# Two-block transformer kernel: the second block's residual in pairs of feature tiles, the sum of squares ahead of the next products, and two moved modulation loads

## The chip, the cores and the metric

The kernel runs on one core of one Trainium2 chip. The metric is device time in microseconds (us), the median over runs. The engines are named as in the profile: PE is TensorE (PEld its weight loads), DVE is VectorE, ACT is ScalarE, POOL is GpSimd, SP is SyncE, which here only issues transfers.

## The reference

512 tokens of 1024 features (and 256 context tokens in the first block) pass through two blocks of two layers, all in fp32. The first block has attention, a Fourier mixer and a Hyena mixer, then a squared-ReLU MLP. The second block, cut to what the change touches, is per layer:

```python
mixed = rms_norm_2(mixer(modulate(rms_norm_2(h, g0), shift, scale)), g1)   # mixer ends in a product with w_out
h = h + gate * mixed
f = rms_norm_2(swiglu_ffn(modulate(rms_norm_2(h, g2), shift2, scale2)), g3)
h = h + gate2 * f
```

where rms_norm_2(x, g) = x * rsqrt(mean(x*x) + 1e-6) * g over the 1024 features. So behind each of the four big products of the second block stands the same tail: a mean of squares of the product y, a residual x + y * gain * r with gain = g * gate per feature and r = rsqrt per token, and a second mean of squares, now of the new x, for the norm ahead of the next product. Layer 0's mixer is HGRN2, layer 1's is dilated attention.

## The kernel before, in words

Activations are feature-major: x is [128 partitions, 8 feature tiles, 512 tokens]. An fp32 product is three matmuls on parts of the operands (mm3: hi by hi at L153, hi by lo at L154 or L155, lo by hi). A weight chunk of 128 x 1024 is loaded raw by SP (wchunk, 3 buffers), its hi part is cast by ACT (L118), its lo part is a subtraction (L119) on POOL, or on DVE for some chunks.

`gemm` takes the output feature tiles m = 0..7 as "head" outputs, once for each part of the tokens: 0:256 and 256:512 (HALVES), or 0:512 and 512:768 in the first block where the context follows the tokens (SEGS). In the first part it takes outputs two at a time, with the eight k steps of the two interleaved, so both chunks' lo parts are wanted almost at once; in a later part, where a function `after` is given, one at a time. `after(s, e)` returns the steps that follow a finished part; they are put on a list, `self.chain`, and `self.link(3)` runs three of them behind each output of the next part. So the first step of a part (`first`: a matmul with a matrix of ones that sums the squares over the partitions, L314, then Ln, Exp, Square on ACT, L318 to L322, and two DVE instructions, L323 and L324, which give r) is emitted behind the first output of the next part. `self.bg(n)` runs n background steps behind an output: loads (L418), products (L424) and finishes (transposes at L433) of the modulation vectors; `bg_flush` runs all that are left.

The order that each engine gets is made from this order of emission by a planner with its own model of durations: an instruction that the model holds ready may be placed ahead of one that it holds not ready. On the chip each engine then runs its list in order.

`resid2` makes the tail of the second block: `first`, then for each of the 8 feature tiles one DVE instruction y * gain * r into a scratch tile (L1340), one add to x (L1341; in the last layer POOL adds tiles 0, 3 and 6), and for the next norm an ACT Square (L290, or L286 for the first) and a DVE add into a running sum (L291). `norm2` follows with three empty steps, its own `first` (of x) and 8 modulate steps (L333, L342, L343), which write the next product's operand u. `proj_out` is the mixer's last product (evacuated by an ACT copy, L1358); `ffn2` ends in `ff_wout` in three chunks of k, of which the last (c == 2) has `after`.

In the first block the first `win` gemm carries background loads and products of modulation vectors in a list that `mod_products` spaces by a gap (3 at L945). The attention output product of layer 0 (`project`, w_out, SEGS) has such a list too, one load of 1 MB (tile mp_w) for each quarter; before it, `load_x` issues the reload of x and of the context from L1065 and L1067.

Of the kernel before, what the change touches and what calls it, by code (L numbers as in the profile page):

```python
# [13 lines left out]
AF = mybir.ActivationFunctionType  # L14
ALU = mybir.AluOpType
# [3 lines left out]
P = 128  # L19
D = 1024  # L20
KD = D // P
L = 512
C = 256
# [56 lines left out]
class Kern:  # L80
# [90 lines left out]
    def gemm(self, srcs, nk, rhs, segs, evac, head=2, parts=None, after=None, n=1024, bg=0, lead=2, dep=False):  # L171

        srcs = list(srcs)
        seg = segs if callable(segs) else (lambda m: segs)
        parts = [(x,) for x in parts] if parts else [seg(0)]
        short = self.xring is None and parts[-1][-1][1] - parts[-1][0][0] <= C

        load = lambda m, short=False: self.wchunk(
            srcs[m], n, extra=self.xring is not None and m > 2,
            lo_eng=self.nc.vector if dep or short and m % 3 == 2 else None)
        head = min(head, len(srcs))
        keep = None  # L190
        if self.xring is not None:

            order = sorted(range(head), key=lambda m: (m not in (3, 4, 5), m)) if dep else range(head)
            keep = {m: load(m) for m in order}
        for part in parts if head else ():
            if dep and part is not parts[0]:
                self.link()
            m0 = 0
            while m0 < head:
                g = lead if m0 == 0 and part is parts[0] else 1 if after and part is not parts[0] else 2  # L200
                ms = range(m0, min(m0 + g, head))
                m0 = ms[-1] + 1
                ws = [keep[m] if keep else load(m, short and part is parts[-1]) for m in ms]
                outs = [[self.psa()[:, : e - s] for s, e in part] for _ in ms]
                for k in range(nk):
                    for w, oo in zip(ws, outs):
                        for (s, e), o in zip(part, oo):
                            self.mm3(o, w[:, k * P : (k + 1) * P], rhs(k)[:, s:e], k == 0, k == nk - 1)
                for m, oo in zip(ms, outs):
                    for (s, e), o in zip(part, oo):  # L210
                        evac(m, s, e, o)
                    if (after or part is parts[-1]) and not (dep and len(parts) > 1):
                        self.bg(bg)
                    self.link(3)
            if after:
                self.link()
                for s, e in part:
                    self.chain += after(s, e)
        for m in range(head, len(srcs)):
            if dep:  # L220
                self.link()
            for (s, e), o in zip(seg(m), self.mtile(self.wchunk(srcs[m], n), nk, rhs, seg(m))):
                evac(m, s, e, o)
            self.bg(bg)
# [662 lines left out]
    def block1_layer(self, l):  # L887
        nc, a = self.nc, self.a
        last = l == 1
# [17 lines left out]
        else:  # L907
# [7 lines left out]
            hvp = ues.enter_context(self.pool("hv", "right"))  # L915
# [26 lines left out]
                      lambda m, s, e, ps: evac(lo + m, s, e, ps), bg=3, **kw)  # L942

        if not last:
            fl, self.bgq = self.bgq, self.mod_products(hvp, "w_mod0", self.bmod[0], (self.m1[0], self.mc[0]), range(2, 4), 3,  # L945
                                                    (hvp, "mp_a"))
            for i, step in enumerate(fl):
                self.bgq.insert(3 * i + 3 * (i > 0), step)
            win(0, 8, tok, evac_hyena, parts=SEGS)
            wes.close()  # L950
            mid = lay.enter_context(self.pool("mid"))
# [14 lines left out]
        if last:  # L966
            hvp = ut
# [57 lines left out]
        else:  # L1025
            p, cat = open_cat()
# [42 lines left out]
        if not last:  # L1069
# [9 lines left out]
            for k in range(4):  # L1079
# [3 lines left out]
            p = tmp.enter_context(self.pool("mods", "right"))  # L1083
            self.bgq += self.mod_products(p, "w_mod0", self.bmod[0], (self.m1[0], self.mc[0]), range(4, 5), 3,
                                          (self.stp, "st_r"))

            def after(s, e):
                if s > 0:
# [231 lines left out]

        return self.norm_to(self.stp, ("b2", l, j), s, self.ng[l][:, 2 * j * KD : (2 * j + 1) * KD], self.m2[l], 3 * j, s, e, LAG)

    def resid2(self, l, j, p, y, sty, s, e):

        nc = self.nc
        last = l == 1 and j == 1
        v = {}

        def first():
            o = (3 * j + 2) * KD  # L1330
            v["r"] = self.stat_rstd(self.stp, sty, D)
            v["g"] = self.cached_gain(("res", l, j), self.ng[l][:, (2 * j + 1) * KD : (2 * j + 2) * KD],
                                      self.m2[l][:, o : o + KD])
            if not last:
                self.st[s] = self.stat_new(self.stp, e - s)

        def tile(k):
            t = self.t(p, [P, C], "r2_t", 3 if last else 2)[:, : e - s]
            x = self.xk(k, s, e)
            nc.vector.scalar_tensor_tensor(t, y[:, k, s:e], v["g"][:, k : k + 1], v["r"], op0=ALU.mult, op1=ALU.mult)  # L1340
            (nc.gpsimd if last and k % 3 == 0 else nc.vector).tensor_tensor(x, x, t, op=ALU.add)  # L1341
            if not last:
                self.stat_add(self.stp, self.st[s], x)
            elif k % 2:
                nc.sync.dma_start(self.a["out"][:, k - 1 : k + 1, s:e], self.x[:, k - 1 : k + 1, s:e])

        return [first] + [lambda k=k: tile(k) for k in range(KD)]

    def proj_out(self, l, key, p, cat):

        nc = self.nc
        y = self.t(p, [P, KD, L], "y")
        sty = {}

        def evac(m, s, e, ps):
            if m == 0:
                sty[s] = self.stat_new(self.stp, e - s)
            nc.scalar.copy(y[:, m, s:e], ps)  # L1358
            self.stat_add(self.stp, sty[s], ps)

        def after(s, e):
            return self.resid2(l, 0, p, y, sty[s], s, e) + self.norm2(l, 1, s, e)

        self.gemm([self.a[key][m] for m in range(KD)], KD, lambda k: cat[k], FULL, evac,
                  head=KD, parts=HALVES, after=after)
        self.link(1 + KD)
# [417 lines left out]
    def ffn2(self, l, es_x):  # L1784
        nc, a = self.nc, self.a
        with self.pool("hid") as hp, self.pool("y") as yp:
# [15 lines left out]
            def evac_out(m, s, e, ps):  # L1802
                if c == 0:
                    nc.scalar.copy(y[:, m, s:e], ps)
                else:
                    nc.vector.tensor_tensor(y[:, m, s:e], ps, y[:, m, s:e], op=ALU.add)
                if c == 2:
                    if m == 0:
                        sty[s] = self.stat_new(self.stp, e - s)
                    self.stat_add(self.stp, sty[s], y[:, m, s:e])  # L1810

            def after(s, e):
                self.bg_flush()
                steps = self.resid2(l, 1, hp, y, sty[s], s, e)
                return steps + self.norm2(1, 0, s, e) if l == 0 else steps

            m0 = 0
# [238 lines left out]
```

## Time and profile before

| what | value |
| --- | --- |
| median of 3 runs | 3510.9 us (3509.56 to 3512.11) |
| the profiled execution | 3506.06 us |
| its span | 3504.3 us |
| instructions | 46813 |
| PE busy | 3287.6 us, 94% of the span |
| DVE, ACT, POOL busy | 57%, 37%, 35% |
| HBM traffic | 106 GB/s over the span |

In the rows further down, a timeline row is: start in us, busy us, engine, line, operation, output<-inputs, shape, count of like instructions that it stands for, and in brackets how long the engine was idle before it and what released it. Starts are from the span's start. A row of the waits says engine, line, what it waited for: us in total, times, longest. "PEclk" is the granted clock of TensorE as a share of full speed.

### The profile page before, as it was taken

Reading aid. Unit: us, or ns where it says so; the run is one execution under the profiler, and the core shown is the slowest. Engines: PE = TensorE matmul, PEld = TensorE weight load, DVE = VectorE, ACT = ScalarE, POOL = GpSimd, SP = SyncE. Lnnn points to the kernel's source line nnn. Section 1 sums busy time; section 2 is a strip of 40 time slices with the busy share of each in tenths; the row PEclk is TensorE's granted clock in tenths of the full one; section 3 lists DMA queues with packets and bytes.
Section 4 is the critical chain, followed back from the end, with each engine's and each line's share of the span. In section 5 each row is a group of like instructions: output and inputs, shape, how many; then the busy total and the mean of one; then the engine's idle time right before and its main releaser. Section 6 shows DMA issues by size and latency. Waiting matters only on the chain. (4 is left out here: it accounts for less than half of the span.)

```text
span 3504.3 us, 46813 instructions
## 1 busy us (share of the span) xinstructions
PE 3287.6 (94%) x18400; PEld 2757.6 (79%) x18400; DVE 2013.0 (57%) x3173; ACT 1288.1 (37%) x2260; POOL 1212.6 (35%) x635
## 2 busy tenths in 40 slices
PE   6988888999998989999999898999989999999998
PEld 2766667888887667888888778888888888898887
DVE  5437748574556557757775666476585474461224
ACT  3235634121123346532245555222423323352222
POOL 2424432222224444234432341344313333313443
PEclk9999999999999999999999999999999999999999
DMA  6330034343433310235542123455323223322332
GB/s 201 127 106 20 29 125 138 109 123 119 133 114 111 98 56 25 90 119 182 185 141 94 55 67 112 150 183 183 100 78 102 91 79 97 97 89 86 95 92 72
DMA packets 150912, 374.32 MB, mean 107 GB/s; under 512 B 18939, under 2 KB 40482, under 8 KB 150692
## 3 DMA queue, kind: packets, MB, share of 16 engines
q1 hardware_dynamic: 146468, 367.14, 32.8%
q10 hardware_dynamic: 4224, 4.19, 0.4%
q8 instruction: 145, 2.38, 0.3%
q14 instruction: 75, 0.61, 0.1%
HBM read 364.98 MB, written 6.29 MB: 106 GB/s over the span
## 5 line engine op out<-in xcount | busy, mean ns | idle before, releaser
L119 POOL TENSOR_TENSOR w_l<-wr,w_h 128x1024 fp32r<-128x1024 f32 (+1 forms) x381 | 915.2, 2404 | 1900.7 <-ACT w_h L118 1891.3
L153 PE MATMUL A<-u_h,w_h 128*128 128x512 f32 (+1 forms) x2344 | 873.6, 374 | 14.5 <-ACT u_h L118 5.0
L155 PE MATMUL A<-u_h,w_l 128*128 128x512 f32 (+1 forms) x2344 | 866.1, 370 | 8.0 <-DVE w_l L119 6.6
L154 PE MATMUL A<-u_l,w_h 128*128 128x512 f32 (+1 forms) x2344 | 866.9, 370 | 1.7 <-DVE u_l L119 1.0
L118 ACT CAST w_h<-wr 128x1024 fp32r<-128x1024 f32 (+1 forms) x406 | 420.3, 1037 | 1100.8 <-PE A L154 745.3
L153 PEld LDWEIGHTS A<-u_h,w_h 128*128 128x128 f32 x2344 | 444.5, 190 | 105.1 <-issue 8.0
L155 PEld LDWEIGHTS A<-u_h,w_l 128*128 128x128 f32 x2344 | 445.2, 190 | 90.6 <-DVE w_l L119 7.7
L154 PEld LDWEIGHTS A<-u_l,w_h 128*128 128x128 f32 x2344 | 445.2, 190 | 82.1 <-DVE u_l L119 1.7
L155 PE MATMUL A<-hid_h,w_l 128*128 128x512 f32 (+1 forms) x1072 | 376.1, 351 | 8.6 <-POOL w_l L119 8.6
L154 PE MATMUL A<-hid_l,w_h 128*128 128x512 f32 (+1 forms) x1072 | 377.6, 352 | 3.1 <-DVE hid_l L119 3.1
L153 PE MATMUL A<-hid_h,w_h 128*128 128x512 f32 (+1 forms) x1072 | 378.6, 353 | 1.4 <-ACT hid_h L118 1.4
L387 DVE SCALAR_TENSOR_TENSOR mo_a<-mo_w,mc_c,mo_a 128x512 f32<-128x512 f32 x266 | 278.4, 1047 | 81.0 <-DMA mo_w<-in_ada_dram 53.4
L155 PEld LDWEIGHTS A<-hid_h,w_l 128*128 128x128 f32 x1072 | 202.8, 189 | 38.5 <-POOL w_l L119 10.7
L154 PEld LDWEIGHTS A<-hid_l,w_h 128*128 128x128 f32 x1072 | 203.2, 190 | 30.9 <-DVE hid_l L119 4.4
L153 PEld LDWEIGHTS A<-hid_h,w_h 128*128 128x128 f32 x1072 | 203.1, 189 | 29.5 <-ACT hid_h L118 2.2
L1799 DVE TENSOR_TENSOR sg<-A,sg 128x512 f32<-128x512 f32 (+1 forms) x52 | 31.4, 607 | 242.6 <-PE A L155 210.0
L1182 DVE SCALAR_TENSOR_TENSOR x<-A,m,x 128x512 f32<-128x512 f32 (+1 forms) x96 | 61.9, 658 | 189.3 <-PE A L155 189.3
L1130 DVE TENSOR_TENSOR relu<-relu 128x512 f32<-128x512 f32 (+1 forms) x104 | 81.3, 810 | 83.9 <-ACT relu L1129 83.9
L1631 DVE TENSOR_TENSOR qk<-A,cos 128x512 f32<-128x512 f32 (+1 forms) x56 | 47.1, 841 | 130.5 <-PE A L155 130.3
L153 PE MATMUL A<-w_h,u_h 128*128 128x256 f32 (+1 forms) x408 | 119.7, 293 | 2.1 <-DVE rt L1634 2.1
L154 PE MATMUL A<-w_l,u_h 128*128 128x256 f32 (+1 forms) x408 | 119.8, 294 | 0.0
L155 PE MATMUL A<-w_h,u_l 128*128 128x256 f32 (+1 forms) x408 | 118.8, 291 | 0.0
(559 smaller groups left out, 6066.0 us busy)
## 6 DMA issues: line engine op xcount, KB each, us to landing
wr<-in_w_mlp_dram SPq DMA_DIRECT2D x139, 512.0 KB, 3.9
mo_w<-in_ada_dram SPq DMA_DIRECT2D x192, 256.0 KB, 2.9
wr<-in_ff_win_dram SPq DMA_DIRECT2D x88, 512.0 KB, 3.7
mo_w<-in_w_mod_dram SPq DMA_DIRECT2D x112, 256.0 KB, 2.8
wr<-in_at_wqk_dram SPq DMA_DIRECT2D x48, 512.0 KB, 3.5
wr<-in_ff_wout_dram SPq DMA_DIRECT2D x32, 512.0 KB, 3.5
wr<-in_w_in_dram SPq DMA_DIRECT2D x30, 512.0 KB, 3.5
mp_w<-in_w_mod_dram SPq DMA_DIRECT2D x12, 1024.0 KB, 5.6
```

The lines of the kernel that those rows point to most:

```text
L118: nc.scalar.copy(dst.hi, src)
L119: (lo_eng or nc.vector).tensor_tensor(dst.lo, src, dst.hi.bitcast(F32), op=ALU.subtract)
L153: ins = mm(out, lhs.hi, rhs.hi, start=first, stop=False)
L154: mm(out, lhs.hi, rhs.lo, start=False, stop=False)
L155: mm(out, lhs.lo, rhs.hi, start=False, stop=last)
L387: nc.vector.scalar_tensor_tensor(state[i], raw, cc[:, k : k + 1], state[i], op0=ALU.mult, op1=ALU.add)
L1130: nc.vector.tensor_tensor(r, r, r, op=ALU.mult)
L1182: nc.vector.scalar_tensor_tensor(x, ps, mod[:, o : o + 1], x, op0=ALU.mult, op1=ALU.add)
L1631: nc.vector.tensor_tensor(d, vw(ps), vw(c), op=ALU.mult)
L1799: nc.vector.tensor_tensor(sgs[s], ps, sgs[s], op=ALU.mult)
```

## The change

The second block's residual takes two feature tiles an instruction and works in y's own place: y *= r (r broadcast over the two tiles), x += y, Square of x into y, and the sum of squares over the pairs, with one 256-wide add at the end; the scratch tile is gone, and the last layer's adds are all on DVE. The gain is applied earlier, when y is evacuated: as the scale of the ACT copy in `proj_out`, and as one more ACT instruction in place in `ffn2`'s last chunk; the table that Ln and Exp use is asked for at the first evacuation. In `gemm`, outputs with `after` are taken one at a time in the first part too (the first group is still `lead`, two), and one chain step is run right behind `after`. In the first `win` the gap of `mod_products` is 2, and in layer 0's `project` the first background step, a load of mp_w, is run ahead of the gemm.

```diff
--- before.py
+++ after.py
@@ -197,7 +197,7 @@
                 self.link()
             m0 = 0
             while m0 < head:
-                g = lead if m0 == 0 and part is parts[0] else 1 if after and part is not parts[0] else 2
+                g = lead if m0 == 0 and part is parts[0] else 1 if after else 2
                 ms = range(m0, min(m0 + g, head))
                 m0 = ms[-1] + 1
                 ws = [keep[m] if keep else load(m, short and part is parts[-1]) for m in ms]
@@ -216,6 +216,8 @@
                 self.link()
                 for s, e in part:
                     self.chain += after(s, e)
+
+                self.link(1)
         for m in range(head, len(srcs)):
             if dep:
                 self.link()
@@ -942,7 +944,7 @@
                       lambda m, s, e, ps: evac(lo + m, s, e, ps), bg=3, **kw)
 
         if not last:
-            fl, self.bgq = self.bgq, self.mod_products(hvp, "w_mod0", self.bmod[0], (self.m1[0], self.mc[0]), range(2, 4), 3,
+            fl, self.bgq = self.bgq, self.mod_products(hvp, "w_mod0", self.bmod[0], (self.m1[0], self.mc[0]), range(2, 4), 2,
                                                     (hvp, "mp_a"))
             for i, step in enumerate(fl):
                 self.bgq.insert(3 * i + 3 * (i > 0), step)
@@ -1084,6 +1086,9 @@
             self.bgq += self.mod_products(p, "w_mod0", self.bmod[0], (self.m1[0], self.mc[0]), range(4, 5), 3,
                                           (self.stp, "st_r"))
 
+
+            self.bgq.pop(0)()
+
             def after(s, e):
                 if s > 0:
                     return []
@@ -1320,31 +1325,42 @@
 
         return self.norm_to(self.stp, ("b2", l, j), s, self.ng[l][:, 2 * j * KD : (2 * j + 1) * KD], self.m2[l], 3 * j, s, e, LAG)
 
-    def resid2(self, l, j, p, y, sty, s, e):
+    def res_gain(self, l, j):
+
+        o = (3 * j + 2) * KD
+        return self.cached_gain(("res", l, j), self.ng[l][:, (2 * j + 1) * KD : (2 * j + 2) * KD], self.m2[l][:, o : o + KD])
+
+    def resid2(self, l, j, y, sty, s, e):
+
+
+
 
         nc = self.nc
+        n = e - s
         last = l == 1 and j == 1
         v = {}
 
         def first():
-            o = (3 * j + 2) * KD
             v["r"] = self.stat_rstd(self.stp, sty, D)
-            v["g"] = self.cached_gain(("res", l, j), self.ng[l][:, (2 * j + 1) * KD : (2 * j + 2) * KD],
-                                      self.m2[l][:, o : o + KD])
-            if not last:
-                self.st[s] = self.stat_new(self.stp, e - s)
-
-        def tile(k):
-            t = self.t(p, [P, C], "r2_t", 3 if last else 2)[:, : e - s]
-            x = self.xk(k, s, e)
-            nc.vector.scalar_tensor_tensor(t, y[:, k, s:e], v["g"][:, k : k + 1], v["r"], op0=ALU.mult, op1=ALU.mult)
-            (nc.gpsimd if last and k % 3 == 0 else nc.vector).tensor_tensor(x, x, t, op=ALU.add)
-            if not last:
-                self.stat_add(self.stp, self.st[s], x)
-            elif k % 2:
-                nc.sync.dma_start(self.a["out"][:, k - 1 : k + 1, s:e], self.x[:, k - 1 : k + 1, s:e])
-
-        return [first] + [lambda k=k: tile(k) for k in range(KD)]
+
+        def pair(k):
+            x, t = self.x[:, k : k + 2, s:e], y[:, k : k + 2, s:e]
+            nc.vector.tensor_tensor(t, t, v["r"].unsqueeze(1).to_broadcast([P, 2, n]), op=ALU.mult)
+            nc.vector.tensor_tensor(x, x, t, op=ALU.add)
+            if last:
+                nc.sync.dma_start(self.a["out"][:, k : k + 2, s:e], x)
+                return
+            nc.scalar.activation(t, x, AF.Square)
+            if k > 0:
+                nc.vector.tensor_tensor(y[:, 0:2, s:e], y[:, 0:2, s:e], t, op=ALU.add)
+            if k == KD - 2:
+                self.st[s] = self.stat_new(self.stp, n)
+                nc.vector.tensor_tensor(self.st[s][0], y[:, 0, s:e], y[:, 1, s:e], op=ALU.add)
+
+        steps = [first]
+        for k in range(0, KD, 2):
+            steps += [lambda k=k: pair(k), lambda: None]
+        return steps
 
     def proj_out(self, l, key, p, cat):
 
@@ -1355,11 +1371,13 @@
         def evac(m, s, e, ps):
             if m == 0:
                 sty[s] = self.stat_new(self.stp, e - s)
-            nc.scalar.copy(y[:, m, s:e], ps)
+                if s == 0:
+                    self.exp_tables()
+            nc.scalar.activation(y[:, m, s:e], ps, AF.Copy, scale=self.res_gain(l, 0)[:, m : m + 1])
             self.stat_add(self.stp, sty[s], ps)
 
         def after(s, e):
-            return self.resid2(l, 0, p, y, sty[s], s, e) + self.norm2(l, 1, s, e)
+            return self.resid2(l, 0, y, sty[s], s, e) + self.norm2(l, 1, s, e)
 
         self.gemm([self.a[key][m] for m in range(KD)], KD, lambda k: cat[k], FULL, evac,
                   head=KD, parts=HALVES, after=after)
@@ -1807,11 +1825,14 @@
                 if c == 2:
                     if m == 0:
                         sty[s] = self.stat_new(self.stp, e - s)
+                        if s == 0:
+                            self.exp_tables()
                     self.stat_add(self.stp, sty[s], y[:, m, s:e])
+                    nc.scalar.activation(y[:, m, s:e], y[:, m, s:e], AF.Copy, scale=self.res_gain(l, 1)[:, m : m + 1])
 
             def after(s, e):
                 self.bg_flush()
-                steps = self.resid2(l, 1, hp, y, sty[s], s, e)
+                steps = self.resid2(l, 1, y, sty[s], s, e)
                 return steps + self.norm2(1, 0, s, e) if l == 0 else steps
 
             m0 = 0
```

## Rows read from the trace of the kernel before

**Rows 1.** The page: busy time, share of the span and instructions of each engine.

```profile
PE 3287.6 (94%) x18400; PEld 2757.6 (79%) x18400; DVE 2013.0 (57%) x3173; ACT 1288.1 (37%) x2260; POOL 1212.6 (35%) x635
```

**Rows 2.** Waits of PE, whole span (what waited <- for what: us, times, longest).

```profile
PE B L314 <- DVE st_h L291: 20.1, 7, 6.5
...
PE A L155 <- DVE w_l L119: 10.1, 4, 4.7
...
PE A L155 <- POOL w_l L119: 9.9, 8, 1.9
...
PE A L424 <- DMA mp_w<-in_w_mod_dram: 8.9, 2, 4.7
```

**Rows 3.** Timeline of PE at the end of the first win stage.

```profile
244.24 1.93 PE L424 MATMUL A<-mp_w,mp_c 128*32 128x256 f32 x16 [4.19 <-DMA mp_w<-in_w_mod_dram]
```

**Rows 4.** Timeline of PE at the start of layer 0's attention output product.

```profile
478.50 1.94 PE L424 MATMUL A<-mp_w,mp_c 128*32 128x256 f32 x16 [4.69 <-DMA mp_w<-in_w_mod_dram]
...
495.85 0.44 PE L433 MATMUL A<-c_ident,st_r 128*128 128x128 f32 x2 [0.97 <-ACT st_r L427]
```

**Rows 5.** Timeline of SP's issues in the same stretch.

```profile
467.96 2.04 SPq L1065 DMA_DIRECT2D x<-in_x_dram  x3
...
470.52 0.43 SPq L418 DMA_DIRECT2D mp_w<-in_w_mod_dram  x1
```

**Rows 6.** Timeline of PE at the end of that product.

```profile
546.92 0.55 PE L153 MATMUL A<-ch_h,w_h 128*128 128x256 f32 x1 [6.21 <-DVE xc L1182]
...
551.34 0.58 PE L155 MATMUL A<-ch_h,w_l 128*128 128x256 f32 x1 [3.44 <-DVE w_l L119]
```

**Rows 7.** Timeline of PE in the first block's last MLP chunk, layer 0.

```profile
1071.28 0.50 PE L155 MATMUL A<-hid_h,w_l 128*128 128x512 f32 x1 [1.16 <-POOL w_l L119]
...
1084.10 0.50 PE L155 MATMUL A<-hid_h,w_l 128*128 128x512 f32 x1 [1.38 <-POOL w_l L119]
...
1135.01 1.22 PE L314 MATMUL B<-st_h,ones 128*128 128x256 f32 x2 [6.47 <-DVE st_h L291]
```

**Rows 8.** Timeline of PE behind HGRN's output product.

```profile
2123.42 0.59 PE L314 MATMUL B<-st_h,ones 128*128 128x256 f32 x2
...
2166.01 1.22 PE L314 MATMUL B<-st_h,ones 128*128 128x256 f32 x2 [5.93 <-DVE st_h L291]
```

**Rows 9.** Timeline of ACT, same place.

```profile
2124.29 1.28 ACT L242 ACT_TABLE_LOAD   x1
```

**Rows 10.** Timeline of DVE, the second half's residual: its start and end.

```profile
2157.17 0.89 DVE L1340 SCALAR_TENSOR_TENSOR r_t<-y,gain,st_rh 128x256 f32<-128x256 f32 x2
2157.97 0.77 DVE L1341 TENSOR_TENSOR x<-x,r_t 128x256 f32<-128x256 f32 x2
...
2165.00 0.95 DVE L291 TENSOR_TENSOR st_h<-st_h,st_sh 128x256 f32<-128x256 f32 x2 [0.21 <-ACT st_sh L290]
```

**Rows 11.** Timeline of PE behind layer 0's last ffn product.

```profile
2496.21 0.39 PE L155 MATMUL A<-hid_h,w_l 128*128 128x256 f32 x1 [1.13 <-POOL w_l L119]
...
2545.98 0.58 PE L155 MATMUL A<-u_h,w_l 128*128 128x256 f32 x1 [4.68 <-DVE w_l L119]
```

**Rows 12.** Timeline of PE behind the dilated attention's output product.

```profile
3124.21 1.22 PE L314 MATMUL B<-st_h,ones 128*128 128x256 f32 x2 [4.04 <-DVE st_h L291]
```

**Rows 13.** Windows behind that wait: busy us (count) by engine, PEclk, DMA share, GB/s.

```profile
3124.00:3130.00 6.00, 5.79 (x26) 5.25 (x27) 2.71 (x8) 4.66 (x9) 0.00 (x0) 0.54 0.00 0
```

**Rows 14.** Timeline of DVE, the last add of the kernel.

```profile
3500.25 0.83 DVE L1341 TENSOR_TENSOR x<-x,r_t 128x256 f32<-128x256 f32 x1
```

**Rows 15.** Groups of DVE, shapes apart: busy us, mean ns | idle before, releasers.

```profile
L291 DVE TENSOR_TENSOR st_f<-st_f,st_sq 128x512 f32<-128x512 f32 x27 | 29.2, 1082 | 53.3 <-ACT st_sq L290 53.1
...
L1512 DVE TENSOR_TENSOR o<-A,nw_r 128x512 f32<-128x512 f32 x8 | 5.5, 691 | 0.6
```

**Rows 16.** The same of ACT.

```profile
L290 ACT ACTIVATE st_sq<-x 128x512 f32<-128x512 f32 x21 | 13.2, 628 | 17.4 <-DVE st_f L291 12.0 <-DMA x<-in_x_dram 5.3
...
L1358 ACT COPY y<-A 128x256 f32<-128x256 f32 x32 | 11.9, 371 | 15.2 <-PE A L155 15.1
```

## The prediction, made before the changed kernel was built or run

> **What bounds the kernel now.** I read the busy line first: PE is busy 94% of the span, every other engine at most 57% [rows 1]. So the time is PE's work plus its idle gaps. The change leaves the three matmuls of each product as they are, so it can only shorten gaps and stretches at a lower clock, or open new ones. All PE gaps together are about 3504.3 - 3287.6 = 217 us; that is the ceiling. Then the waits of PE [rows 2]: the matmul that sums the squares waits for DVE's running sum seven times, 20.1 us in all; products wait for a weight's lo part 20.0 us (10.1 from DVE, 9.9 from POOL); two products of modulation vectors wait 8.9 us for their load. Most of this stands at the ends of stages, where the next product needs the norm of what the last has just written. Then I read PE's timeline at each such end [rows 3, 4, 6 to 8, 11, 12], and the engine that was late there. Shares over the whole span say nothing of these places: DVE, 57% busy on the whole, is the bound inside them.
>
> One of these is a chain by itself. In the second half's residual DVE runs from 2157.17 to 2165.95 almost without a stop (idle 0.21), 8.8 us, and PE waits 5.93 us for its last add [rows 8, 10]. [...]
>
> **Part by part.** All sums are against the profiled execution, 3506.06 us (span 3504.3 and 1.8 around it), which is 4.8 us under the median of 3510.9.
>
> *Gap 2 in the first win stage.* PE waits 4.19 us for the load of the last modulation product, which nothing covers [rows 3]. The list with gap 3 is longer than the steps that the gemm's outputs call, so its end is flushed, load and product back to back. With gap 2 it is 8 steps shorter and fits, and the load lies beside products. I take -4.2; bounds 0 (the load is late all the same) and -5.2 (with the 16 small matmuls at full clock, half of 1.93).
>
> *The first load of layer 0's project.* PE waits 4.69 us for it [rows 4]. SP issues it at 470.52, behind three reloads of x that began at 467.96 (0.68 us each) and one of the context; those wait for the memory to come free [rows 5]. Emitted ahead of the weight loads it stands behind two of them: the issue moves by about 470.52 - 469.3 = 1.2 us and the transfer has less beside it. I take -2; bounds 0 and -4.69. Three finishes there wait about 1 us each for the copy of their rows (one in rows 4). With outputs one by one, two of them fall behind a whole product: -2, bounds 0 and -3.
>
> *The sum step ahead of the next products.* At the end of this project PE waits 6.21 and 3.44 us for the context's residual and for a lo part, both on DVE, which has the modulates of the first part between them [rows 6]. The first part's `first` comes up to one output earlier. I take -3 of the 9.65; bounds 0 and -6. The last MLP chunk of layer 0 has the same form: a wait of 6.47 us for the sum of the second part [rows 7], -3, bounds 0 and -6.5.
>
> *Outputs one at a time.* Where two chunks are wanted at once, the second's lo part comes late by 1.16 and 1.38 us [rows 7], 1.13 us [rows 11], and once more like that in layer 1's ffn: -4.7 for the four. Those of each gemm's first group, which stays two, remain. Bounds 0 and -7.
>
> *The residual in pairs.* By starts, a tile costs DVE about 0.40 (0.80 for two L1340) and twice 0.335 for the adds, 8 x 1.07 = 8.6 us a half [rows 10]. After: per pair two 512-wide instructions, three 512-wide adds of squares, one 256-wide. No row has a 512-wide add of two SBUF operands in quiet; one with a PSUM operand took 0.691, one of two SBUF operands beside POOL's lo parts 1.082 [rows 15]. A start-to-start saving of 0.1 as in the rows of 256 gives 0.60: 11 x 0.60 + 0.34 = 6.9. At the end the last pair's Square (0.63 [rows 16]) and two adds come in a row, 0.3 longer than now. So -1.4 a half by 0.60 (nearest to the row without contention), and 11 x 1.08 + 0.34 = 12.2, so +3.6 a half, by the other end.
>
> Behind HGRN's output product two more things come off: the table load of 1.28 us on the way from the sum to r [rows 9], and the later emission. The second half's r is made between modulates of the first half, so when the first half is earlier the second half's is too. I take -4 of the 5.93; behind the dilated product, with no table load in the way, -2.8 of 4.04 [rows 12]; behind layer 0's ffn, where the wait of 4.68 us is for a lo part queued on a full DVE [rows 11], -2.5. Bounds for the three: 0 and -14.6 below, +3.6 each, 10.8 above.
>
> *The gain in the evacuation.* The copy of 0.371 us [rows 16] takes a pointer; in `ffn2` 32 more ACT instructions of the same size come, 32 x 0.4 = 13 us of ACT work, beside products that last 3 to 6 us each; ACT is 37% busy. Taken as 0; without that cover at a part's last output it is 0.4 us at each of four parts, 1.6.
>
> *The tail.* The last add ends at 3501.08, on DVE [rows 14]. Four pairs of two 0.60 us instead of 8 multiplications and five adds on DVE, and no POOL: -1.4; bounds 0 and -2.
>
> *The clock.* Five of the waits named above are followed by some 6 us at about half clock. A stretch like rows 13 costs 5.79 x 0.46 = 2.7 us; shorter waits, of which some will not be followed by a fall: -6 of some 13, bounds 0 and -13.
>
> *What is added.* `first` ahead of the next products puts the sum matmul in PE's list right behind the part's last product. It needs that product's evacuation (0.37), Square (0.39) and add (0.43), 1.2 us. While it waits, the next part's first product is behind it on PE, and everything else behind that. At eight part ends the planner can still let products overtake it, by its own durations; I take 0.6 each, +4.8. Bounds 0, and 8 x 2.5 = 20 where DVE's adds take the 1.08 of rows 15 and stand behind others.
>
> Sum: -4.2 - 2 - 2 - 3 - 3 - 4.7 - 4 - 2.8 - 2.5 - 1.4 - 6 + 4.8 = -30.8. From 3506.1 that is 3475.3 us for a profiled execution; a median 4.8 above it is 3480.
>
> **Rivals.** *DVE stays the bound at the half changes (A).* What is removed from the chain is filled with lo parts and modulates that were waiting; PE waits as long, under another name. For it: at rows 11 the wait is for a lo part on DVE, not for the residual. Against it: rows 8 and 12 wait for the running sum itself. Then the waits on loads and pairs (-4.2 - 4.7 - 2) and the tail (-1.4) stay, the rest is 0: -12, about 3499.
>
> *The pairs are stretched beside POOL (B).* A 512-wide add with two SBUF operands takes 1.08 in the mean beside POOL's lo parts [rows 15], and in the pairs every instruction on DVE is one. Price +3.6 instead of -1.4 at seven halves if POOL is at work in all: 7 x 5 = +35, of which PE feels those where DVE is the wait, about three: +15; 3495. Against it: the chain of rows 10 ran at full pace. [...]
>
> *The sum step blocks PE (C), the other side.* At each part's end PE stands in order before the sum matmul, and the running sum's last add stands in DVE's list behind modulates and lo parts that are there already, so the wait isn't 1.2 us but like those of rows 2, 20.1 / 7 = 2.9 in the mean and up to 6.5; say 4 at eight ends, +32, and behind each a stretch at half clock, 2.7 as in rows 13, +21.6: +53.6 in the place of +4.8, with the rest as above: -35.6 + 53.6 = +18, about 3529. It decides for slower from (35.6 + 7) / 8 = 5.3 us an end, clock included. For it: the seven waits of rows 2. Against it: at 2123.42 the sum matmul had no wait [rows 8], DVE is free there, and the planner can place products ahead.
>
> *All of it comes (D).* Gaps close to the bounds and the clock stays up: -45 to -55, about 3460.
>
> **How the numbers follow.** Forecast (-20 to -40) 0.45; A and B 0.27; D 0.12; nothing visible 0.08; C 0.08. Gains and losses under 0.2% (7 us) are about what a measurement of this kernel can't tell from no change. Faster: 0.45 + 0.27 + 0.12 = 0.84; same 0.08; slower 0.08. The range from 3456 to 3506 leaves out C, half of "nothing visible" and the far end of D.
>
> **What would show it.** The load wait at 244 gone; the one at 478 at 2 to 3 us; pair waits on POOL's lo parts down to those of first groups; the waits for the running sum from 20 to about 10 us; 512-wide DVE instructions of the residual at 0.65 to 0.75 us, no table load between a sum matmul and its Ln; the granted clock higher behind the half changes. Wrong would be: sum matmuls that wait 2 us or more right behind a part's last product (C), new waits on DVE's lo parts of the old length (A), or residual instructions above 1 us (B).

## The result, and the profile after

The changed kernel takes 3475.2 us (median of 4 runs, 3473.3 to 3476.3) against 3510.2 us for the kernel before beside it: a ratio of 0.990 (0.9883 to 0.9917), -35 us. The forecast was 3480, range 3456 to 3506. The profiled execution took 3476.3 us with a span of 3474.4, so from profile to profile it is -29.7 us where the sum said -30.8; from median to median it is -35. A second series of the same kernel gave 3474.0 against 3510.9, ratio 0.990 (0.9881 to 0.9914), and a profile with a span of 3469.0. The 5.4 us between those two profiles lie almost wholly ahead of the 750th matmul (4.87), where the very first weight loads scatter.

First the page's busy line of the changed kernel, then PE's waits (waited <- for: us, times, longest), answering to [rows 1, 2].

```profile
PE 3283.4 (95%) x18400; PEld 2758.8 (79%) x18400; DVE 2004.0 (58%) x3097; ACT 1303.9 (38%) x2268; POOL 1207.9 (35%) x629
```

```profile
PE B L316 <- DVE st_h L1358: 11.2, 4, 5.5
PE A L155 <- DVE w_l L119: 10.7, 3, 5.2
...
PE A L153 <- DVE xc L1187: 8.2, 2, 4.1
...
PE A L155 <- POOL w_l L119: 5.3, 5, 1.2
...
PE B L316 <- DVE st_h L293: 3.8, 4, 1.9
...
PE A L426 <- DMA mp_w<-in_w_mod_dram: 3.4, 1, 3.4
```

PE is busy 4.2 us less with the same 18400 matmuls (mean granted clock 0.980 against 0.978), and idle less by the rest of the span. The waits for the running sum fell from 20.1 to 15.0 us, half of the way to the 10 us that the prediction named as a sign; those for loads of mp_w fell from 8.9 to 3.4, those for POOL's lo parts from 9.9 to 5.3. Those for DVE's lo parts (10.1 to 10.7) and for the context's residual (8.6 to 8.2) hardly moved. In the second profile the wait for the load of mp_w is 2.0 us instead of 3.4.

To place the saving, I took the start of the same-numbered matmul in every trace (all have 18400) and the differences from the kernel before, stage by stage. This table is worked out from the traces; stages that no edit touches are left out.

| us against the kernel before | to #750 | first win's end, to #1250 | project, #1750 to 2500 | last MLP chunk, #4500 to 5750 | HGRN output, #10500 to 11500 | ffn 0, #12500 to 13500 | dilated output, #16000 to 17000 | last ffn, #18000 to 18399 | tail | span |
| --- | --- | --- | --- | --- | --- | --- | --- | --- | --- | --- |
| changed kernel | +3.2 | -7.0 | -6.1 | -7.1 | -6.4 | -3.1 | -3.4 | +1.7 | -1.3 | -29.9 |
| the same, second profile | -1.7 | -6.7 | -6.6 | -8.3 | -6.3 | -2.6 | -3.6 | +1.8 | -1.4 | -35.3 |
| one_loads | +2.6 | -7.0 | -3.4 | -1.7 | +1.0 | 0.0 | 0.0 | +0.1 | 0.0 | -7.9 |
| one_single | -1.4 | -0.9 | -2.9 | -6.5 | +0.4 | 0.0 | +0.7 | +0.2 | 0.0 | -9.6 |
| one_link | +1.3 | -0.1 | +0.3 | -0.1 | -3.3 | -1.1 | +0.3 | +0.5 | +0.1 | -2.2 |
| one_resid_b | -0.9 | -1.0 | +0.2 | -1.9 | -3.5 | -2.0 | -3.4 | +1.4 | -1.4 | -12.1 |
| one_table | +0.9 | +2.2 | +0.4 | -1.7 | -2.3 | +0.5 | -0.2 | +1.4 | 0.0 | +2.0 |
| after_nolink | +0.3 | -7.0 | -6.0 | -6.7 | -5.7 | -2.0 | -4.6 | 0.0 | -1.1 | -31.7 |
| after_lead1 | +2.9 | -7.8 | -5.7 | -9.7 | -6.0 | +0.3 | -3.5 | +2.4 | -1.3 | -28.3 |
| after_loadfirst | +4.5 | -7.3 | -8.2 | -7.0 | -6.1 | -2.8 | -3.6 | +1.9 | -1.3 | -26.4 |
| after_lopool | +5.8 | -7.1 | -5.5 | -7.2 | -6.1 | -2.5 | -3.3 | +1.9 | -1.3 | -24.3 |
| after_deppool | +2.7 | -7.4 | -9.7 | -6.8 | -3.6 | +2.6 | -3.6 | +0.4 | -1.4 | -24.3 |

Read it with its scatter, which kernels that do not touch a stage show: 6 us up to #750; 2.2 at the first win's end (one_table); in the last MLP chunk 1.9 (the -1.7 to -1.9 of three kernels) and 2.6 (after_lead1 against the changed kernel); up to 2.4 in the last ffn (below); up to 1 at the others. Sizes below that are not findings, and each row is one profile.

### The profile page after: what moved, and what is told of

The parts are those of the page before. It is cut to its first block, busy times and chain, and to the rows that moved or that the text cites. A ratio compares the mean times of both kernels' runs of the same rounds, so it can differ in the third digit from the quotient of the medians.

```text
span 3474.4 us, 46674 instructions
## 1 busy us (share of the span) xinstructions
PE 3283.4 (95%) x18400; PEld 2758.8 (79%) x18400; DVE 2004.0 (58%) x3097; ACT 1303.9 (38%) x2268; POOL 1207.9 (35%) x629
## 3 DMA queue, kind: packets, MB, share of 16 engines
q10 hardware_dynamic: 4224, 4.19, 0.4%
## 5 line engine op out<-in xcount | busy, mean ns | idle before, releaser
L154 PEld LDWEIGHTS A<-hid_l,w_h 128*128 128x128 f32 x1072 | 204.4, 191 | 30.8 <-DVE hid_l L119 4.3
```

The source lines that it names most:

```text
L154: mm(out, lhs.hi, rhs.lo, start=False, stop=False)
```

## The experiments

**One part alone.** Four kernels, each the kernel before with one part of the change, and a fifth, one_table, with a piece of the last part.

one_loads:

```diff
-... range(2, 4), 3,
+... range(2, 4), 2,
+            self.bgq.pop(0)()
```

> The kernel before with only the two moved modulation loads (gap 2 in the first win stage; the first background step of layer 0's project ahead of its gemm). Theory (each load's wait is cut where it stands, and nothing behind moves): the wait of 4.19 us at 244 is gone, the one of 4.69 us at 478 falls to about 3.4 as in the changed kernel, so -5 to -7 us. Rival (the earlier loads only push the weight loads behind them, so a product waits instead): new waits on wr or on lo parts of together 3 to 5 us, and the time within 2 us of before.

Measured: ratio 0.9972 (0.9959 to 0.9984), some -10 us; by stages -7.0 at the first win's end and -3.4 at project. The theory's mechanism held, and it gave more than its -5 to -7 us: the wait at 244 is gone, and the one at 478 fell from 4.69 to 2.34 us, with the 16 matmuls behind it at 1.07 us instead of 1.94. No weight load took the place of the two.

one_single:

```diff
-g = lead if m0 == 0 and part is parts[0] else 1 if after and part is not parts[0] else 2
+g = lead if m0 == 0 and part is parts[0] else 1 if after else 2
```

> The kernel before with only the outputs taken one at a time in the first part where after is given. Theory: the pair waits in the last MLP chunk (1.16 and 1.38 us) and those of about 1 us on the modulation finishes in project go, those of 1.13 us in the second block's ffn stay as they did in the changed kernel, because there a 256-wide output takes less time than POOL's lo part of its chunk: -4 to -7 us in all. Rival (the waits in ffn are the pairs' too, and something else in the changed kernel brought them back): they are gone here, and it is -7 to -9.

Measured: 0.9977 (0.9967 to 0.9987), -8 us: -2.9 at project, -6.5 in the last MLP chunk (some 1.8 of it scatter), nothing in the second block. The theory held, also for the waits in ffn, which stayed, and the last MLP chunk gave more than it said, because a third pair wait, of 1.86 us, went too.

one_link:

```diff
                     self.chain += after(s, e)
+                self.link(1)
```

> The kernel before with only the one chain step right behind a part's last output. Theory (the earlier sum of squares is what shortens the half changes): the waits for the running sum and for DVE at the ends of project, mlp2, the two output products and ffn shorten by 6 to 12 us in all. Rival (DVE is the bound there and the shorter residual made the room): within 3 us of before. Second rival (PE stands in order before the sum matmul): 3 us or more slower.

Measured: 0.9994 (0.9985 to 1.0003), the same time. The theory fell and the second rival too: nothing at project and the last MLP chunk, -3.3 and -1.1 in the second block, no loss anywhere. The total is the first rival's, but the -3.3 at HGRN's output is more than the scatter, so the earlier sum is worth something there by itself.

one_resid has all edits of the second block: the pairs, the gain in the evacuation and the early table. one_resid_b is the same kernel once more, and its stages are read from there.

```diff
-            nc.vector.scalar_tensor_tensor(t, y[:, k, s:e], v["g"][:, k : k + 1], v["r"], ...)
...
+            nc.vector.tensor_tensor(t, t, v["r"].unsqueeze(1).to_broadcast([P, 2, n]), op=ALU.mult)
+            nc.vector.tensor_tensor(x, x, t, op=ALU.add)
...
-            nc.scalar.copy(y[:, m, s:e], ps)
+            nc.scalar.activation(y[:, m, s:e], ps, AF.Copy, scale=self.res_gain(l, 0)[:, m : m + 1])
```

> The kernel before with only the second block's residual in pairs, the gain in the evacuation and the table asked for at the first evacuation. Theory (DVE's chain at the second half is shorter by 1.4 us and the table load is off the way): in the second block -5 to -9 us, of it 1.4 in the tail; nothing in the first block. Rival (the earlier sum is what counts): -1.4 in the tail and less than 2 us besides. Rival (the pairs are stretched beside POOL): residual instructions of about 1.1 us and no gain.

> The same kernel as one_resid, for a profile by stage. Theory (pairs and table make their own room): by the start of stages, HGRN's output product to ffn -3 us, ffn of layer 0 to the dilated attention -2 to -3, the dilated output product -3, the tail -1.3. Rival (the earlier sum makes what is won there): below 1 us at each, apart from the tail.

Measured: 0.9971 (0.996 to 0.9982), -10 us; by stages -3.5, -2.0, -3.4 and -1.4 in the tail, as the theory said.

one_table:

```diff
             if m == 0:
                 sty[s] = self.stat_new(self.stp, e - s)
+                if s == 0:
+                    self.exp_tables()
```

> The kernel before with only the table of Ln and Exp asked for at the first evacuation of the two products. Theory (the load of 1.28 us lay on the way to r at two places): -1 to -2.5 us by the starts of stages, at HGRN's output product and layer 0's ffn; nothing behind the dilated product, where no load stood. Rival (the first half's r has slack, the second half's chain is what PE waits for): 0.

One profile: -2.3 at HGRN's output, nothing at ffn (+0.5) and the dilated product (-0.2). One of the two places, so the theory held by half. By this one profile most of the pairs' -3.5 at HGRN's output is the table's, while at ffn and the dilated product the pairs themselves pay.

The spans of the three larger parts, -7.9, -9.6 and -12.1, add up to -29.6, against -29.9 and -35.3 in the two profiles of the whole. Without the stretch up to #750, which scatters by itself, the three give -29.9, with one_link -33.3, and the whole -33.0 and -33.6. So the parts add up within a few us over the whole span. That they are independent is not shown: at HGRN's output the three give +1.0, +0.4 and -3.5 alone and -5.7 together (after_nolink).

**One part undone or moved further in the changed kernel.**

after_nolink:

```diff
-                self.link(1)
```

> The changed kernel without the chain step right behind a part's last output. Theory (that step pays only in the second block, where the residual in pairs is too): nothing in the first block, +3 to +5 us at HGRN's output product and layer 0's ffn together. Rival (it pays with outputs one at a time, in the last MLP chunk): +3 or more there. Second rival (with the shorter residual it is not wanted): within 1 us everywhere.

Measured: 0.9904 (0.9889 to 0.9919), 3476.6 us: the same as the changed kernel. +0.7 and +1.0 at HGRN's output and ffn, -1.3 at the dilated product. The second rival is nearest: with the shorter residual the step is hardly wanted, though in the kernel before it gave 3.3 us at HGRN's output.

after_lead1:

```diff
-... after=after, n=kc * P, bg=2)
+... after=after, n=kc * P, bg=2, lead=1)
```

> The changed kernel with the first group of ffn's last chunk also one output wide. Theory (the wait of 1.13 us for a lo part, forecast to go with the pairs, belongs to the first group, which stayed two): it goes in both layers, -2 us together. Rival (POOL's lo part of 2.4 us is slower than a 256-wide output of some 2.2 us, whatever the groups): the wait stays near 1 us or moves to the next output, and the time is the same.

Measured: 0.9906 (0.989 to 0.9923), 3478.0 us, the same. PE's timeline at the start of that chunk in layer 0, the changed kernel first and then after_lead1:

```profile
2464.82 0.39 PE L155 MATMUL A<-hid_h,w_l 128*128 128x256 f32 x1 [0.95 <-POOL w_l L119]
2470.04 0.39 PE L154 MATMUL A<-hid_l,w_h 128*128 128x256 f32 x1 [0.40 <-DVE hid_l L119]
2472.26 0.39 PE L155 MATMUL A<-hid_h,w_l 128*128 128x256 f32 x1 [1.13 <-POOL w_l L119]
```

```profile
2466.27 0.80 PE L153 MATMUL A<-hid_h,w_h 128*128 128x256 f32 x2 [2.85 <-ACT hid_h L118]
2467.80 0.58 PE L154 MATMUL A<-hid_l,w_h 128*128 128x256 f32 x1 [0.30 <-DVE hid_l L119]
```

Both waits on lo parts, 0.95 and 1.13, are gone, but only the first one belonged to the first group. An output is 24 matmuls here (8 steps of k, three each), which take 2.9 us from 2472.20 on in after_lead1, where the expectation here has 2.2 and that of one_single less than POOL's lo part, which takes 2.44 in the mean of the changed kernel. Counted in the trace, the wait of 0.95 stands at the 6th matmul of the chunk and the one of 1.13 at the 51st, which is the first lo part of the third output. POOL, in the changed kernel, has that lo part ready only at 2472.20:

```profile
2469.39 2.81 POOL L119 TENSOR_TENSOR w_l<-wr,w_h 128x1024 fp32r<-128x1024 f32 x1
```

In after_lead1 PE comes to the 51st matmul later, because the other operand holds it first. The last step of k needs the hidden activation that ACT casts; with one output in the group PE is there after 21 matmuls instead of 42, and waits 2.85 us. In the 5.73 us from 2466.27, behind that wait, its granted clock is 0.50, and its matmuls start 0.21 us apart, against 0.12 from 2472.20 on. So the stage of layer 0's ffn is 3.3 us slower than in the changed kernel, by a mechanism that neither named.

after_loadfirst:

```diff
-            for k in range(2):
-                load_x(k)
...
             self.bgq.pop(0)()
+            for k in range(2):
+                load_x(k)
```

> The changed kernel with the two reloads of x and their places ahead of project's gemm issued behind the first load of modulation weights instead of ahead of it. Theory (what is left of the wait at 473, 3.42 us, is the bytes of the two reloads that go first and share the engines, and 0.9 us of issue): -1.5 to -3 us at project, its wait 0.5 to 2 us. Rival (the load waits for its place in memory, which comes free only then, and its own 1 MB is the rest): the issue stays at about 465 and the wait above 3 us.

SP's issues in the changed kernel, then SP's and PE's rows in after_loadfirst:

```profile
464.07 0.85 SPq L1067 DMA_DIRECT2D x<-in_x_dram  x2
464.98 0.43 SPq L420 DMA_DIRECT2D mp_w<-in_w_mod_dram  x1
```

```profile
433.64 0.39 SPq L420 DMA_DIRECT2D mp_w<-in_w_mod_dram  x1
...
465.40 1.48 SPq L1067 DMA_DIRECT2D x<-in_x_dram  x2
```

```profile
471.19 1.07 PE L426 MATMUL A<-mp_w,mp_c 128*32 128x256 f32 x16
473.74 0.44 PE L435 MATMUL A<-c_ident,st_r 128*128 128x128 f32 x2 [1.49 <-ACT st_r L429]
```

Neither theory had it. The load is issued 31 us earlier and the wait of 3.42 us is gone: its own place had long been free, and it stood in SP's list behind two reloads that wait for x's place. By matmul 2000, counted from #1750, the kernel is 3.9 us ahead of the changed one; at #2500 2.1 of it is left and at #4500 0.8. Part of the loss is a lower granted clock: from matmul 2300 to 2400 it is 0.74 against 0.80, with PE busy 16.25 us against 14.87. Against the second profile of the changed kernel, where the load's wait is 1.96 us, it is 2.0 us ahead at matmul 2000 and 0.3 at #4500. The profiled execution, 3479.8 us, is the slowest of its four. The time, 3471.8 us, ratio 0.9888 (0.9871 to 0.9904), is the lowest median measured, but its interval overlaps the changed kernel's: faster than it by 3 us or equal, not settled.

after_lopool:

```diff
-lo_eng=self.nc.vector if dep or short and m % 3 == 2 else None)
+lo_eng=self.nc.vector if dep else None)
```

> The changed kernel with every third lo part of the context's outputs in layer 0's project and last MLP chunk on POOL too, not on DVE. Theory (DVE is full there, 12.0 us of 12, and PE waits 4.13 and 5.15 us for what is queued on it): the wait for DVE's lo part of 5.15 us falls by 1 to 4 us at mlp2 and the time of that stage by 1 to 3. Rival (POOL's 2.4 us a chunk is slower than a 256-wide output, and a busy POOL stretches DVE's 512-wide modulates to 2.8 us): the same or up to 4 us slower there.

Measured: 0.9905 (0.9887 to 0.9924), 3478.5 us, the same. PE's timeline of the last MLP chunk's end, changed kernel first:

```profile
1095.67 0.38 PE L153 MATMUL A<-hid_h,w_h 128*128 128x256 f32 x1 [0.87 <-ACT w_h L118]
1100.30 0.55 PE L153 MATMUL A<-hid_h,w_h 128*128 128x256 f32 x1 [4.13 <-DVE xc L1187]
1106.43 0.58 PE L155 MATMUL A<-hid_h,w_l 128*128 128x256 f32 x1 [5.15 <-DVE w_l L119]
1120.62 0.70 PE L316 MATMUL B<-st_h,ones 128*128 128x256 f32 x2 [1.93 <-DVE st_h L293]
```

That kernel's waits there add up to 12.1 us. In after_lopool they are 1.68, 1.95, 2.00 and 6.39 us, 12.0 in all, on other names. The rival's outcome, and by its mechanism: DVE is full there (12.00 of 12 us from 1095 in the changed kernel), and the lo parts that were taken off it, 1.2 us each, stretch its modulates from POOL. In after_lopool, DVE and then POOL:

```profile
1101.70 3.50 DVE L335 SCALAR_TENSOR_TENSOR md_t<-x,gain,st_r 128x512 f32<-128x512 f32 x2
...
1111.92 0.74 DVE L335 SCALAR_TENSOR_TENSOR md_t<-x,gain,st_r 128x512 f32<-128x512 f32 x1
```

```profile
1101.89 2.75 POOL L119 TENSOR_TENSOR w_l<-wr,w_h 128x1024 fp32r<-128x1024 f32 x1 [2.33 <-ACT w_h L118]
```

Of the 3.50 us for two, one took 2.84, the one beside POOL's lo part. An estimate, from the durations above the median of the same instruction without POOL beside it: from 1085 to 1125 seven of DVE's instructions are stretched by 13.7 us together, in the changed kernel from 1085 to 1121 six by 10.7.

after_deppool is after_loadfirst with more on POOL (the line shown is the new part):

```diff
-lo_eng=self.nc.vector if dep or ...
+lo_eng=self.nc.vector if dep and (keep is None or m not in (3, 4, 5)) or ...
```

> The changed kernel with the first load of project ahead of the reloads of x, and with three of the eight lo parts of the second block's first weight chunks behind each half change on POOL instead of DVE. Theory (DVE is what PE waits for there: 3.45 us behind HGRN's output product, 5.54 behind layer 0's ffn, 2.02 behind the dilated product; POOL is idle): these waits fall by 4 to 7 us together and the second block by 3 to 6 by the starts of stages; with the load some -3 to -7 in all against the changed kernel. Rival (the waits are for the chain of the residual itself, which no lo part delays): the waits within 1 us of the changed kernel's. Second rival (POOL's lo parts stretch the residual's 512-wide instructions beside them from 0.69 to 1.1 us or more, or come late themselves): new waits on POOL's lo parts, and the second block the same or slower.

> The changed kernel once more, on the same chip and beside the same runs of the kernel before, as the measure for the version with the load first and the lo parts on POOL: 31 to 38 us below the kernel before by every theory.

Measured together: after_deppool 3482.2 us, 0.9919 (0.9904 to 0.9933), after_again 3474.0, 0.9897 (0.9881 to 0.9914). The theory fell: against the second profile of the changed kernel +2.7 at HGRN's output and +5.1 at ffn. PE's timeline of after_deppool behind layer 0's ffn:

```profile
2510.15 1.22 PE L316 MATMUL B<-st_h,ones 128*128 128x256 f32 x2 [3.90 <-DVE st_h L1358]
2523.51 0.50 PE L153 MATMUL A<-u_h,w_h 128*128 128x256 f32 x2 [1.04 <-ACT u_h L344]
2538.85 1.22 PE L316 MATMUL B<-st_h,ones 128*128 128x256 f32 x2 [4.67 <-DVE st_h L1358]
```

The old wait (5.54 in the changed kernel) fell only to 4.67, and the first half's sum got one of 3.90 that was not there. The second rival's reason is the cause of the new wait. DVE's rows and then POOL's, just ahead of it:

```profile
2504.82 2.46 DVE L1355 TENSOR_TENSOR y<-y 128x512 f32<-128x512 f32 x1 [1.11 <-ACT y L1353]
...
2507.54 2.56 DVE L1358 TENSOR_TENSOR st_h<-y 128x256 f32<-128x256 f32 x1
```

```profile
2504.34 2.38 POOL L119 TENSOR_TENSOR wx_l<-wr,wx_h 128x1024 fp32r<-128x1024 f32 x1 [23.34 <-ACT wx_h L118]
2507.22 2.60 POOL L119 TENSOR_TENSOR wx_l<-wr,wx_h 128x1024 fp32r<-128x1024 f32 x1 [0.49 <-ACT wx_h L118]
```

The last two adds of the first half's sum ran beside POOL's moved lo parts and took 2.46 and 2.56 us, where the changed kernel has 0.69 and 0.42: 3.9 us more together, which is PE's wait. The mean over the residual's instructions hides it, because the other 81 of 128x512 met no lo part and stayed at 0.68 to 0.70. At HGRN's output three other DVE instructions are stretched to 2.07 to 2.62 us, and PE has a new wait of 2.83 us for a lo part on DVE; that the one comes of the others is likely and not shown.

## Why the prediction was right, point by point

**The loads.** Predicted -4.2 and -2 (and more by the clock). The first win's end gave -7.0 in the changed kernel and in one_loads alike: 4.19 us of wait, and the smaller waits and half-clock products around it (the granted clock is 0.50 from 237 to 247 in the kernel before; the 16 matmuls of [rows 3] take 1.07 us in the changed kernel). So that term was mis-sized by 2.8. The second load's wait fell by 1.27 (4.69 to 3.42) in the first profile and by 2.73 (to 1.96) in the second, 2.35 (to 2.34) in one_loads: about the 2 that was taken. The cause that I gave for what is left, that the transfer shares the engines, is not the main one: after_loadfirst shows that SP's order holds the issue back by 31 us. Whether sharing has a part in what separates 3.42 from 1.96 is open.

**The finishes.** Predicted -2: of three waits of about 1 us one is left (0.83), -2.2.

**The sum step.** Here the prediction failed, with two terms that nearly cancelled. I took -3 at project and -3 in the last MLP chunk for the earlier sum, and +4.8 for PE standing before it. one_link shows neither. At the end of project the waits of 6.21 and 3.44 [rows 6] became 4.12 and 5.15, in one_link and in the changed kernel alike; the latter's rows:

```profile
535.93 0.55 PE L153 MATMUL A<-ch_h,w_h 128*128 128x256 f32 x1 [4.12 <-DVE xc L1187]
...
542.05 0.58 PE L155 MATMUL A<-ch_h,w_l 128*128 128x256 f32 x1 [5.15 <-DVE w_l L119]
```

That is 9.65 and 9.27 in all, the same DVE work under other names, which was rival A. In the last MLP chunk of one_link the sum's wait fell from 6.47 to 4.91 and the stage took the same time. Behind layer 0's ffn it is A as well: the wait of 4.68 for a lo part [rows 11] is one of 5.54 for the running sum now, though smaller waits beside it (1.71 and 1.55) are gone and the stage is shorter. And the sum matmul of y, which rival C would have had waiting, found its operand ready: behind the second block's four big products it waits 0.20 us at most, apart from the kernel's last one (1.43, and 1.49 before). Behind HGRN's output product the first half's two sums, of y and of the new x, stand without a wait in PE's timeline of the changed kernel, and the second half's of x waits 3.45 where it waited 5.93 [rows 8]:

```profile
2103.43 0.70 PE L316 MATMUL B<-st_h,ones 128*128 128x256 f32 x2
2114.64 0.70 PE L316 MATMUL B<-st_h,ones 128*128 128x256 f32 x2
...
2142.06 0.72 PE L316 MATMUL B<-st_h,ones 128*128 128x256 f32 x2 [3.45 <-DVE st_h L1358]
```

**Outputs one at a time.** Predicted -4.7 from four waits of pairs. In the last MLP chunk 1.16 and 1.38 went, and with them 1.86 at the second group of two, which I had left out: 4.4 us, of which the waits behind them took 1.1 back (10.99 to 12.08). The two of 1.13 in ffn stayed, because I took them for a pair's second lo part. They are the first lo part of the third output, at the 51st matmul, which POOL has ready 1.1 us after PE comes to it, whether the outputs are taken by two or by one.

**The residual in pairs.** Predicted 0.60 from start to start, -1.4 a half. The groups of DVE and of ACT in the changed kernel (mean ns behind the busy time), and DVE's timeline of the second half, answering to [rows 10]:

```profile
L1349 DVE TENSOR_TENSOR x<-x,y 128x512 f32<-128x512 f32 x32 | 20.8, 684 | 0.0
L1348 DVE TENSOR_TENSOR y<-y,st_rh 128x512 f32<-128x512 f32 x32 | 20.8, 686 | 0.3
L1355 DVE TENSOR_TENSOR y<-y 128x512 f32<-128x512 f32 x18 | 12.4, 686 | 0.6 <-ACT y L1353 0.2
```

```profile
L1831 ACT ACTIVATE y<-y,gain 128x256 f32<-128x256 f32 x32 | 16.1, 509 | 0.9
L1376 ACT ACTIVATE y<-A,gain 128x256 f32<-128x256 f32 x32 | 15.0, 470 | 12.3 <-PE A L155 12.2
```

```profile
2133.50 1.29 DVE L1348 TENSOR_TENSOR y<-y,st_rh 128x512 f32<-128x512 f32 x2
...
2138.92 1.22 DVE L119 TENSOR_TENSOR wx_l<-wr,wx_h 128x1024 fp32r<-128x1024 f32 x1
2140.06 1.49 DVE L1355 TENSOR_TENSOR y<-y 128x512 f32<-128x512 f32 x2
2141.58 0.42 DVE L1358 TENSOR_TENSOR st_h<-y 128x256 f32<-128x256 f32 x1
```

Two take 1.29, so 0.60 from start to start, as taken. Rival B did not come: 0.68 to 0.69 us in 82 instructions. But its condition did not come either: by the starts and ends in the trace, not one of the 82 ran while POOL was at work, so they say nothing of what POOL would do to them; after_deppool does, with 2.46 and 2.56 us. The chain itself, 2133.50 to 2142.00, is 8.5 us and only 0.3 shorter than before, because a lo part of 1.14 us now stands in it; without it, 7.4. So part of what was won on DVE was used by work that had waited. The stages still gave -6.4, -2.6 to -3.1 and -3.4 to -3.6, where -4, -2.5 and -2.8 were taken, with the clock's share apart. The gain on ACT costs 0.10 us a copy and 32 new instructions of 0.51; no wait of PE names them. I had taken 0.4 for each of these.

**The tail.** Predicted -1.4, measured -1.34, and the same in every kernel with the pairs (after_nolink, -1.05, apart).

**The clock.** Predicted -6. PE's busy time with the same matmuls fell by 4.2. The last ffn gave 1.7 of it back without any new gap: PE was granted 0.88 in 3410 to 3422 of the changed kernel and 1.00 in 3440 to 3452 of the one before. Of the nine rows above with the early table seven lose 1.4 to 2.4 us there, and the three without it 0.1 to 0.5; but after_nolink (0.0; 1.00 in that stretch) and after_deppool (0.4) have the table and don't. What sets it off is open.

So the sum was right to 1 us from profile to profile, and that closeness is luck: two profiles of the one changed kernel are 5.4 us apart, the medians moved by 35, and the parts were off both ways. The waits in ffn and the sum step were mis-sized by +2.2, +6 and -4.8, the first win's end and the HGRN stage by some -3 and -2.

## What to carry to other kernels

Where a stage's end is held by one full engine, an earlier place for the sum that PE waits for renames the wait (project, one_link); fewer and wider instructions on that engine shortened it in the second block. Moving some of its work to POOL did not: the DVE instructions that were stretched beside POOL's lo parts took 1.3 to 2.2 us longer each, where a lo part had cost DVE 1.2. So see what will run beside what before moving work there, and read single rows, since a group's mean hides a single long instruction. Before pricing a late load, look at what stands ahead of it in the issuing engine's list: the load here waited 31 us behind reloads whose destination was busy, while its own was free. And a part's profile, compared by the start of the same-numbered matmul, separates effects of some 1 to 2 us where the times themselves scatter by 3 and more.

## What was not expected of the hardware

DVE's pace beside POOL. In the changed kernel the 512-wide adds of the first block's running sum took 0.69 us where no POOL instruction ran at the same time (14 of 27) and 0.80 to 2.55 where one did (13). An estimate over the whole trace, from the durations above the median of the same instruction without POOL beside it: 276 of DVE's instructions are longer by more than 0.1 us, by some 395 us together, out of 2004 us busy.

In one stretch two profiles of the one changed kernel differ by the granted clock alone: from matmul 8740 to 8760 the second loses 1.1 us to the first with no gap in PE. Shortly ahead of it PE waits alike in both, 1.41 us and then 1.72 or 1.73. The windows of these matmuls, the changed kernel's first profile and then its second (us, busy (count) of PE, PEld, DVE, ACT and POOL, PEclk, DMA share, GB/s):

```profile
1790.45:1792.92 2.47, 2.47 (x23) 2.47 (x22) 2.47 (x4) 1.49 (x4) 2.47 (x2) 1.00 0.55 169
```

```profile
1783.83:1787.41 3.58, 3.58 (x22) 3.58 (x21) 3.21 (x4) 1.47 (x2) 3.58 (x3) 0.65 0.74 239
```

PE was busy all through both and was granted 1.00 in the one and 0.65 in the other. And with a group of two in ffn, the second output's matmuls covered a wait of 2.85 us on ACT that no row showed until the group was made one wide (after_lead1).
